# The last 512 output columns of a decode step computed with the tokens as the stationary operand

## The chip, the cores and the metric

The kernel runs on one core of a Trainium2 chip. A core has TensorE (PE in the profile; PEld is its loading of the stationary operand), VectorE (DVE), ScalarE (ACT), GpSimd (POOL) and SyncE (SP), which run side by side and wait for each other by semaphores. SP, ACT and POOL also issue DMAs between HBM and the on-chip memory SBUF; all DMAs share 16 engines. Matmul results land in PSUM, in banks of 512 fp32 numbers a partition. The metric is the device time of one execution in microseconds (us); the median over a few runs is compared.

## The reference, cut to what matters

One layer with three groups of heads (short convolution, sparse attention over a paged cache, attention over a memory) is computed for 256 prompt tokens and for 8 sequences with 4 new tokens each, 288 tokens in all. What the change touches is the end:

```python
    mixed = jnp.concatenate([y_a, y_b, y_m], axis=-1)
    return x + mixed @ w_out, kv_new, win_state, conv_new

def rms_norm(x, g):
    xf = x.astype(jnp.float32)
    y = xf * lax.rsqrt(jnp.mean(xf * xf, axis=-1, keepdims=True) + NORM_EPS)
    return (y * g.astype(jnp.float32)).astype(x.dtype)

    y_prompt = rms_norm(xp, final_g)
    y_sample = rms_norm(xs, final_g)
```

`mixed` is 288 tokens by 2048, `w_out` is 2048 by 2048, and the final norm needs the sum of squares over all 2048 output columns of a token before any column of it can be scaled.

## The kernel before

**Layout.** Everything is kept with features on the 128 partitions and the 288 tokens (`NT`: 0 to 127 and 128 to 255 prompt, 256 to 287 decode) along the free dimension. A matrix product is made tile by tile: 128 output columns at a time, with the weights as the stationary operand (128x128) and the 288 tokens as the moving one. The weights come in halves of 128 x 1024 numbers, eight 128x128 blocks each, numbered `s`; `wsrc` lists them in the order in which they are used. To hold fp32 accuracy at the speed of the rounded format fp32r, each operand is split into a rounded part and a rest: `w_load` (L215, DMA from POOL, five buffers `w`), `w_hi` (L222, ACT copy to `wh`, three buffers), `w_lo` (L227, DVE subtraction to `wl`, two buffers). `product_half` (L244) then issues 24 matmuls of 288 columns for a half: high by high, high by low and low by high for eight blocks.

**Order.** There is no scheduler: instructions stand on each engine in the order in which the Python code issues them. Side work (attention of the decode tokens, residual, squares) is written as generators; `chunk` (L159) lets each that is due take one step, twice in each half.

**The output projection.** It runs in two passes over 16 tiles of 128 output columns, since half of the 2048 rows of `mixed` are ready earlier than the other half. The first pass (L1484) multiplies rows 0 to 1023 (`y1`, the split form) and ACT copies each result to `ysum` (`first_pass`, L1429). `residual` (L1434) loads the input x in six pieces through SP and DVE adds it. The second pass (L1490) multiplies rows 1024 to 2047 (`y2`); in `second_pass` (L1458) DVE adds the PSUM tile to `ysum`, ACT squares it, DVE adds the squares to `yacc`, and ACT multiplies the tile by the norm's gain `fg`, in place.

**The tail.** After the last tile the squares are summed over partitions by matmuls with a column of ones (`sum_tokens`, L1452, tile `ssqy`), `rsqrt` (L197) makes the factor of each token in one ACT and five small DVE instructions, three matmuls (`spread_tokens`) spread the 288 factors over all partitions (tile `rb`), and DVE multiplies `ysum` by them in seven pieces (`OUT_PIECES`); each piece is stored as soon as it is done, from ACT and SP in turn (L1500 to L1503). `busy` (L1443) issues matmuls whose results nobody reads.

Of the kernel before, what the change touches and what calls it, by code (L numbers as in the profile page):

```python
# [9 lines left out]
F32 = mybir.dt.float32  # L10
# [8 lines left out]
D = 2048  # L19
KT = 16  # L20
# [49 lines left out]
DIRECT = 4  # L70
WARM = 3
LOW_FIRST = 22
TAIL_BUSY = (5, 7)
OUT_PIECES = (1, 2, 2, 3, 3, 3, 2)


@with_exitstack
def decode_step(ctx, tc, xT, xN, xD, memT, cst, w_in, w_mem, w_out, w_bg, pt, ptv, ckc, ckk, ckv, wk, wv, mk, mv,
                o_y, o_kv, o_mem, o_conv, o_wk, o_wv):
    nc = tc.nc  # L80
    pool = lambda name, bufs, **kw: ctx.enter_context(tc.tile_pool(name=name, bufs=bufs, **kw))
# [28 lines left out]
    def matmul(out, a, b, **kw):  # L110
        n = size(out)
        k, t = ((0, n / 2400 + 0.0115) if b.dtype == F32R else (1, n * 0.00048 + 0.008) if out.shape[0] == 32
                else (2, max(0.21, n * 0.00143)))
        if k != kind[0]:
            at[0] += 0.2 if 1 in (k, kind[0]) else 0.08
        kind[0] = k
        at[0] += t
        nc.tensor.matmul(out, a, b, **kw)  # L118
# [37 lines left out]
    def spawn(gen, delay=0):  # L156
        live.append([now[0] + delay, gen])
# [22 lines left out]
    def small(w, name, bufs=2):  # L180
        return psm.tile([128, w], F32, name=name, tag=name, bufs=bufs)
# [9 lines left out]
    def C(name):  # L191
        o, w = _COFF[name]
        return c[:, o:o + w]

    ident = C("ident")

    def rsqrt(r, ssq):  # L197

        v, t = small(3, "yv", 1)[:, :r.shape[1]], small(3, "yt", 1)[:, :r.shape[1]]
        act.activation(r, ssq, AF.Sqrt, scale=1.0 / D, bias=C("eps"))  # L200
        vec.tensor_scalar(v, ssq, 1.0 / D, EPS, op0=ALU.mult, op1=ALU.add)
# [9 lines left out]
    wsrc += [half(w_out[i], j) for j in range(2) for i in range(16)]  # L211
    raws, his, los = {}, {}, {}
    NH = len(wsrc)

# [12 lines left out]
    def w_lo(s, eng=None):  # L227
        if DIRECT <= s < NH and s not in los:
            los[s] = pw.tile([128, 1024], F32R, name=f"wl{s}", tag="wl", bufs=WL)
            (eng or vec).tensor_tensor(los[s], raws.pop(s), his[s].bitcast(F32), op=ALU.subtract)  # L230
# [1198 lines left out]
    def first_pass(n, z):  # L1429
        act.activation(ysum[:, n, :], z, AF.Copy)  # L1430
        return
        yield

    def residual():  # L1434
        for n in range(0, 16, 3):
            m = min(3, 16 - n)
# [6 lines left out]
    def busy(n):  # L1443

        for _ in range(n):
            matmul(rb[:, :NT], y2[:, 0, 0:128], y2[:, 0, :], start=True, stop=True)

    acc = zt("C", "yacc")
    rb = pss.tile([128, 512], F32, name="rb", tag="s")
    ssq = pss.tile([128, 512], F32, name="ssqy", tag="s")  # L1450

    def sum_tokens(sq, first):  # L1452
        for i, (o, _) in enumerate(GROUPS):
            matmul(ssq[:, i:i + 1], sq[:, o:o + 128], C("ones"), start=(first and i == 0), stop=(not first and i == 2),
                   skip_group_check=True)


    def second_pass(n, z):  # L1458
        y = ysum[:, n, :]
        vec.tensor_tensor(y, z, y, op=ALU.add)  # L1460
        if n < 15:
            yield 1
        if n == 0:
            act.activation(acc, y, AF.Square)
        else:
            s = zt("B", "ysq")
            if n < 15:
                act.activation(s, y, AF.Square)
                vec.tensor_tensor(acc, acc, s, op=ALU.add)
            else:  # L1470
                act.activation(s[:, :128], y[:, :128], AF.Square)
                vec.tensor_tensor(s[:, 128:], y[:, 128:], y[:, 128:], op=ALU.mult)
                busy(TAIL_BUSY[0])
                sum_tokens(s, False)
# [3 lines left out]
        if n == 14:  # L1478
            yield 1
            sum_tokens(acc, True)  # L1480

    spawn(split_prompt(), 2)
    spawn(split_decode(), 1)
    for n in range(16):  # L1484
        if n == 12:
# [4 lines left out]
    for n in range(16):  # L1490
        then(second_pass(n, product([(lambda j: y2[:, j, :], lambda j: y2[:, 8 + j, :])], NT)))
    while live:
        idle()

    r = small(3, "yr")
    rsqrt(r, ssq[:, 0:3])
    busy(TAIL_BUSY[1])
    spread_tokens(rb, r, GROUPS)
    n = 0
    for i, m in enumerate(OUT_PIECES):  # L1500
        yv = ysum[:, n:n + m, :]
        vec.tensor_tensor(yv, yv, rb[:, :NT].unsqueeze(1).to_broadcast([128, m, NT]), op=ALU.mult)
        (nc.sync if i % 2 else nc.scalar).dma_start(o_y[:, n:n + m, :], yv)  # L1503
        n += m

# [47 lines left out]
def _inputs(x_prompt, x_sample, cache_kv, cache_win, state_conv, cache_mem, page_table, mem_prompt,  # L1553
# [17 lines left out]
    wcat = np.concatenate([q, mq] + parts + conv + [mg, ng], 1)  # L1571
    wbg = np.concatenate([bg, np.zeros((D, 8), w.dtype)], 1).reshape(KT, 128, 32).transpose(1, 0, 2)
    wo = np.concatenate([w_out[0][0:512], w_out[0][1536:2048], w_out[0][512:1536]], 0)
    ck = cache_kv[0]
    ckc = ck[:, :, 0:2].transpose(0, 4, 2, 3, 1).reshape(160, 128, 512)
    ckk = ck[:, :, 2].transpose(0, 3, 2, 1).reshape(160, 128, 256)
# [10 lines left out]
    return dict(xT=A(tr(x)), xN=A(x[:NTP]), xD=A(x[NTP:].reshape(NTS, 4, 512).transpose(1, 0, 2).reshape(128, 512)),  # L1587
                memT=A(np.concatenate([vec(mem_norm_g), tr(mem_prompt.reshape(256, D)).reshape(128, KT * 256)], 1)), cst=A(cst), w_in=A(_ktiles(wcat)),
                w_mem=A(_ktiles(w_mem_kv[0])), w_out=A(_ktiles(wo)), w_bg=A(wbg), pt=A(pt), ptv=A(ptv), ckc=A(ckc), ckk=A(ckk), ckv=A(ckv),
                wk=A(wk), wv=A(wv), mk=A(mk), mv=A(mv))  # L1590


_OUTS = dict(o_y=(128, KT, NT), o_kv=(12, 128, NT), o_mem=(8, 128, 256), o_conv=(128, 72), o_wk=(4, 2, 128, 1024),
             o_wv=(2, 4, 128, 1024))


def _outputs(r):
    y = r["o_y"].transpose(1, 0, 2).reshape(D, NT)
# [7 lines left out]
    return (A(y[:, :NTP].T).reshape(1, NTP, D), A(y[:, NTP:].T).reshape(8, 4, D), A(kv[:NTP, 0:4])[None, None],  # L1606
            A(kv[:NTP, 4:6])[None, None], A(conv[0:2])[None, None],
            A(r["o_mem"].reshape(2, 4, 128, 256).transpose(3, 0, 1, 2))[None, None],
            A(kv[NTP:, 0:4]).reshape(1, 8, 4, 4, 2, 128), A(win)[None], A(conv[2:18]).reshape(1, 8, 2, 512))
# [15 lines left out]
```

## Time and profile before

| what | us |
|---|---|
| runs | 617.47, 617.70, 618.82; median 617.7 |
| the profiled execution, as timed | 617.0 |
| its span from first to last instruction | 614.7 |
| TensorE busy, of the span | 600.8 (98%) |
| VectorE busy | 459.1 (75%) |
| ScalarE busy | 285.8 (46%) |
| mean granted TensorE clock | 0.992 |

The span is that of the core's instructions and DMAs; 2.3 us of the timed execution lie outside it. Busy time counts an instruction from its start to its end, so that overlapping instructions of a pipeline are counted once; a matmul's own duration in the profile is longer than the distance to the next one. In rows of the trace in order of time the columns are the start, the duration of the row, engine, source line, operation, output and inputs, tile sizes, and xN for the number of instruction records in it. A matmul on plain fp32 operands leaves two records, one on fp32r operands one.

### The profile page before, as it was taken

To read this page: it belongs to the slowest core of one execution; us is meant where nothing else is said; L and a number is where in the kernel's file an instruction comes from. 1 tells how busy PE (TensorE), PEld (TensorE's weight loads), DVE (VectorE), ACT (ScalarE), POOL (GpSimd) and SP (SyncE) were. 2 spreads that over 40 slices of the span, in tenths; PEclk is the share of its full clock that TensorE was granted. 3 is DMA by queue.
4 is the path that set the end of the run, shared out by engine and by line. 5 is a ranking of instruction groups with operands and counts; after the bars stand their busy time and mean duration, and the time that the engine had idled before them with its cause. 6 is when DMAs were issued, how large, how long until landed. Compare 5 with 4: busy or idle time off the path is not lost.

```text
span 614.7 us, 13334 instructions
## 1 busy us (share of the span) xinstructions
PE 600.8 (98%) x4893; PEld 558.6 (91%) x4893; DVE 459.1 (75%) x737; ACT 285.8 (46%) x500; POOL 200.8 (33%) x282
## 2 busy tenths in 40 slices
PE   8999999999999999999999999999999999999993
PEld 6999999989999999888998989889898898999993
DVE  5789799988576599997987879897568533357754
ACT  4755545544464345325435434443544444346650
POOL 2012545434235342324465523331212364122200
PEclk8999999999999999999999999999999999999998
DMA  8999798999988998898888898989898888677623
GB/s 315 388 405 401 255 326 306 333 297 378 338 266 305 347 399 341 295 384 293 292 314 275 312 361 279 304 284 337 290 362 327 326 290 307 227 256 280 231 85 154
DMA packets 75217, 188.40 MB, mean 307 GB/s; under 512 B 8784, under 2 KB 26352, under 8 KB 74896
## 3 DMA queue, kind: packets, MB, share of 16 engines
q0 software_dynamic: 26048, 100.48, 45.5%
q1 hardware_dynamic: 47808, 84.98, 38.9%
q10 hardware_dynamic: 1296, 2.11, 0.9%
q8 instruction: 38, 0.62, 0.4%
q14 instruction: 27, 0.22, 0.1%
HBM read 182.31 MB, written 13.60 MB: 319 GB/s over the span
## 4 chain that ended last, share of the span: by engine, by line
PE 84%; DVE 7%; DMA 6%; issue 1%; SPq 1%; ACT 0%; ACTq 0%; DVEq 0%
PE z L118 65%; PE od L118 3%; DMA st<-ckc 3%; PE sk L118 3%; PE zf L118 2%; DVE pooled L135 2%; PE acc L118 2%; PE s L118 2%; DMA rx<-xT 1%; DVE wl L135 1%; DVE st L135 1%; PE pt L123 1%; DVE ysum L135 1%; DMA mraw<-memT 1%; PE pv L123 1%
## 5 line engine op out<-in xcount | busy, mean ns | idle before, releaser
L118 PE MATMUL z<-x,wh 128*128 128x288 f32 x1664 | 254.4, 302 | 0.0
L135 DVE TENSOR_TENSOR wl<-w,wh 128x1024 fp32r<-128x1024 f32 x148 | 185.6, 1255 | 86.4 <-PE z L118 43.4
L118 PEld LDWEIGHTS z<-x,wh 128*128 128x128 f32 x1664 | 229.8, 188 | 7.8 <-issue 6.1
L135 ACT ACTIVATE wh<-w 128x1024 fp32r<-128x1024 f32 x148 | 154.4, 1052 | 20.3 <-PE z L118 14.4
L118 PE MATMUL z<-x,wl 128*128 128x288 f32 x832 | 127.0, 295 | 0.3 <-DVE wl L135 0.3
L118 PEld LDWEIGHTS z<-x,wl 128*128 128x128 f32 x832 | 115.7, 188 | 0.5 <-DVE wl L135 0.5
L350 POOL TENSOR_TENSOR st<-st,cst 128x512 f32<-128x512 f32 x63 | 69.7, 1108 | 129.5 <-issue 58.5
L219 POOL DMA_DIRECT2D w<-w_in x104 | 58.2, 560 | 108.6 <-DVE wl L135 79.2
L135 DVE TENSOR_REDUCE pooled<-st 128x16 f32<-128x1024 f32 x63 | 76.2, 1210 | 5.8 <-POOL st L350 5.8
L135 DVE TENSOR_TENSOR st<-st,cst 128x512 f32<-128x512 f32 x63 | 43.8, 697 | 8.8 <-DMA st<-ckc 8.7
L219 POOL DMA_DIRECT2D w<-w_out x32 | 17.5, 550 | 64.4 <-DVE wl L135 43.6
L578 POOL DMA_INDIRECT st<-ckv,rows_v x26 | 27.0, 1040 | 32.2 <-PE od L118 17.6
L118 PE MATMUL z<-y,wh 128*128 128x288 f32 x256 | 37.0, 297 | 0.0
L118 PE MATMUL z<-y1a,wh 128*128 128x288 f32 x224 | 35.4, 298 | 0.0
L118 PEld LDWEIGHTS z<-y,wh 128*128 128x128 f32 x256 | 35.1, 188 | 0.0
L118 PEld LDWEIGHTS z<-y1a,wh 128*128 128x128 f32 x224 | 31.4, 188 | 2.1 <-issue 1.2
L118 PE MATMUL z<-m,wh 128*128 128x256 f32 x192 | 27.3, 287 | 0.5 <-DVE mvt L135 0.5
L135 ACT ACTIVATE P<-P,nm 128x128 f32<-128x128 f32 (+1 forms) x32 | 14.2, 446 | 27.7 <-DVE nm L135 27.7
L118 PEld LDWEIGHTS z<-m,wh 128*128 128x128 f32 x192 | 24.7, 191 | 0.8 <-issue 0.7
L135 ACT ACTIVATE ysum<-z 128x288 f32<-128x288 f32 x16 | 6.6, 412 | 35.2 <-PE z L118 33.4
L118 PE MATMUL z<-y,wl 128*128 128x288 f32 x128 | 19.6, 296 | 0.0
L118 PE MATMUL z<-y1a,wl 128*128 128x288 f32 x128 | 19.5, 295 | 0.0
(286 smaller groups left out, 692.0 us busy)
## 6 DMA issues: line engine op xcount, KB each, us to landing
w<-w_in POOLq DMA_DIRECT2D x104, 512.0 KB
st<-ckc SPq DMA_DIRECT2D x126, 256.0 KB, 5.5
w<-w_out POOLq DMA_DIRECT2D x32, 512.0 KB
st<-ckk SPq DMA_DIRECT2D x112, 128.0 KB, 4.9
w<-w_mem SPq DMA_DIRECT2D x12, 512.0 KB
o_wk<-wk POOLq DMA_DIRECT2D x8, 512.0 KB
o_wv<-wv POOLq DMA_DIRECT2D x8, 512.0 KB
st<-mv SPq DMA_DIRECT2D x7, 512.0 KB, 7.8
```

The lines of the kernel that those rows point to most:

```text
L118: nc.tensor.matmul(out, a, b, **kw)
L123: nc.tensor.transpose(out, a, b)
L135: return getattr(self.engine, name)(*args, **kw)
L219: (nc.gpsimd if s >= ON_SYNC else nc.sync).dma_start(raws[s], wsrc[s])
L350: done.append(eng.tensor_tensor(tm[:, :, kv], tm[:, :, kv], acmp[:, kv].unsqueeze(1).unsqueeze(1).to_broadcast([128, 2, 4, 64]), op=ALU.mu ...
L578: nc.gpsimd.indirect_dma_start(t, None, ckv, bass.IndirectOffsetOnAxis(ap=rows_v[:, j * 4 + b:j * 4 + b + 1], axis=0))
```

## The change

The last 512 output columns (4 of the 16 tiles) are taken out of both passes, which now run over `DT` = 12 tiles.

- **First pass.** After 12 tiles, `first_rows` makes the product of `y1` with the last 512 columns: the stationary operand is a 128x128 block of tokens, the moving one is 512 columns of the weights. `rows` issues six matmuls of 512 columns for a half of the weights and a group of 128 tokens; there are four halves and the two prompt groups. DVE adds the residual, which is loaded in this layout into `ysum` ahead of time (`xL`). The decode tokens are left out here.
- **Second pass.** After 12 tiles the same is done with `y2`, group 0 first. Each prompt group then has its own sum of squares (the 12 tiles by `yacc` as before, the 512 columns by an ACT square that also sums along the row), its own `rsqrt`, its own spreading matmul, four scaled pieces (three on DVE with four tiles each, one on ACT with the 512 columns) and four stores.
- **Decode tokens.** Their 32 rows of the last 512 columns are computed at the end in plain fp32, from unsplit weights, by 64 matmuls that write 32 partitions and 128 columns each (`decode_rows`; tile `zd`, 4 quarters of the columns on 4 quarters of the partitions). Four weight halves of the first pass are loaded again for it, into buffers `st` that the attention no longer uses; the other four are still in `w`.
- The output array has another layout in HBM, group by group; the host side puts it together.

```diff
+    def first_rows():
+        z = row_tiles()
+        y = y1["hi"], y1["lo"]
+        for p in range(4):
+            s, w = next_weights()
+            for g in range(2):
+                rows(z[g], w, 2 * p, y, g, p == 0, p == 3)
...
+    def rows(z, w, k, y, g, first, last):
+        wh, wl = w
+        hi, lo = y
+        mm = [(a(k + i)[:, 128 * g:128 * g + 128], w[:, i * ROWS:(i + 1) * ROWS])
+              for a, w in ((hi, wh), (lo, wh), (hi, wl)) for i in range(2)]
+        for i, (a, b) in enumerate(mm):
+            matmul(z, a, b, start=first and i == 0, stop=last and i == 5)
...
-    for n in range(16):
-        if n == 12:
-            spawn(residual())
+    for n in range(DT):
+        if n == 8:
+            nc.sync.dma_start(yl, xL)
         then(first_pass(n, product([(y1["hi"], y1["lo"])], NT)))
+    spawn(residual())
+    first_rows()
...
+    for n in range(DT):
+        if n in (2, 3, 4, 5):
+            wr[n - 2] = buffers[n - 1]
+            nc.sync.dma_start(wr[n - 2], wsrc[NH - 20 + n - 2])
+        elif n == 6:
+            nc.sync.dma_start(buffers[0][:, :640], fgl)
+        then(second_pass(n, product([y2hl], NT)))
...
+    def decode_rows(a, b):
+        for k in range(a, b):
+            for q in range(4):
+                o = (k % 2) * ROWS + 128 * q
+                matmul(zd[32 * q:32 * q + 32, :128], mixed[:, k, 256:NT], wr[k // 2][:, o:o + 128],
+                       start=(k == 0), stop=(k == KT - 1), skip_group_check=True)
...
+    squares(0, z[0])
+    gains(0)
+    r0 = factors(0, sums2[:, 0:1])
+    scale_rows(0, r0, nc.sync)
+    rows(z[1], ws[0], 2, y, 1, False, False)
+    rows(z[1], ws[1], 4, y, 1, False, False)
+    spread_rows(0, r0)
+    rows(z[1], ws[2], 6, y, 1, False, True)
+    scale_tiles(0, 0, 4, nc.sync)
+    scale_tiles(0, 4, 8, nc.sync)
+    squares(1, z[1])
+    scale_tiles(0, 8, 12, nc.sync)
+    gains(1)
+    r1 = factors(1, sums2[:, 1:2])
+    scale_rows(1, r1, nc.scalar)
+    decode_rows(0, SPREAD_AT)
+    spread_rows(1, r1)
+    decode_rows(SPREAD_AT, KT)
+    scale_tiles(1, 0, 4, nc.sync)
+    squares(2, zd[:, :128])
+    busy(TAIL_BUSY[0])
+    matmul(ssq[:, 3:4], sel, sums2[:, 2:3], start=True, stop=True)
+    scale_tiles(1, 4, 8, nc.sync)
+    gains(2)
+    scale_tiles(1, 8, 12, nc.sync)
+    r2 = factors(2, ssq[:, 3:4])
     busy(TAIL_BUSY[1])
-    spread_tokens(rb, r, GROUPS)
...
+    spread_rows(2, r2)
+    scale_rows(2, r2, nc.scalar)
+    scale_tiles(2, 0, 12, nc.sync)
```

`squares` adds a finished PSUM group to `ysum` (DVE) and squares it with a sum (ACT); `gains` multiplies by the gain (DVE); `factors` is `rsqrt`; `scale_rows` scales the 512 columns on ACT and stores them; `scale_tiles` scales four tiles on DVE and stores them.

On TensorE, at the end of the program, these instructions stood last before the change (`z` is the PSUM tile, the number behind `wh` and `wl` tells one half of the weights from another, `y` is y2):

```order
L118 MATMUL z_7556<-y_6383,wh_7487 128x288 x16
L118 MATMUL z_7556<-y_6383,wl_7525 128x288 x8
L118 MATMUL z_7588<-y_6383,wh_7523 128x288 x12
L118 MATMUL ssqy<-cst,yacc 128x1 x3
L118 MATMUL z_7588<-y_6383,wh_7523 128x288 x4
L118 MATMUL z_7588<-y_6383,wl_7557 128x288 x8
L118 MATMUL rb<-y_6383 128x288 x5
L118 MATMUL ssqy<-cst,ysq 128x1 x3
L118 MATMUL rb<-y_6383 128x288 x7
L118 MATMUL rb<-cst,yr 128x128 x2
L118 MATMUL rb<-cst,yr 128x32
```

On TensorE, from the last three halves of group 0 and group 1 on, there now stand these (`zr_0` and `zr_1` are the two groups' PSUM tiles, `zd` the decode tokens', `idl` the tile that nobody reads):

```order
L120 MATMUL ssqy<-cst,both 128x1
L120 MATMUL zr_0_7434<-wh_7464,y_6383 128x512 x4
L120 MATMUL zr_0_7434<-wl_last,y_6383 128x512 x2
...
L120 MATMUL rb<-cst,yr_7496 128x128
L120 MATMUL zr_1_7435<-wh_7464,y_6383 128x512 x4
L120 MATMUL zr_1_7435<-wl_last,y_6383 128x512 x2
L120 MATMUL zd<-st_105,mixed 32x128 x8
...
L120 MATMUL zd<-w_7316,mixed 32x128 x4
L120 MATMUL rb<-cst,yr_7535 128x128
...
L120 MATMUL zd<-w_7352,mixed 32x128 x8
L120 MATMUL idl<-y_6383 128x288 x4
...
L120 MATMUL rb<-cst,yr_7625 128x32
```

The one spreading of factors behind all products has become three: group 0's stands ahead of group 1's last half, group 1's inside the decode tokens' matmuls, and only that of the decode tokens' 32 factors stands last.

On VectorE the program ended so before (`wl` is the subtraction for the last half, `ysum<-ysum,rb` the scaling of the output):

```order
L135 TENSOR_TENSOR wl_7557<-w_7406,wh_7523 128x1024
L135 TENSOR_TENSOR ysum<-z_7556,ysum 128x288
L135 TENSOR_TENSOR yacc<-yacc,ysq 128x288
L135 TENSOR_TENSOR ysum<-z_7588,ysum 128x288
L135 TENSOR_TENSOR ysq<-ysum 128x160
L135 TENSOR_SCALAR yv<-ssqy 128x3
L135 RECIPROCAL yr<-yr 128x3
...
L135 TENSOR_TENSOR ysum<-ysum,rb 128x288
L135 TENSOR_TENSOR ysum<-ysum,rb 128x576 x2
L135 TENSOR_TENSOR ysum<-ysum,rb 128x864 x3
L135 TENSOR_TENSOR ysum<-ysum,rb 128x576
```

On VectorE the stretch from group 1's factors to the end now reads (`yo` and `yod` are the output buffers, `st_104` holds the gains):

```order
L137 SCALAR_TENSOR_TENSOR yr_7535<-yt,yr_7535 128x1
L137 TENSOR_TENSOR yo<-ysum,rb 128x512
L137 TENSOR_TENSOR ysum<-zd,ysum 128x128
L137 TENSOR_TENSOR yo<-ysum,rb 128x512
L137 TENSOR_TENSOR yod<-ysum,st_104 128x128
L137 TENSOR_TENSOR yo<-ysum,rb 128x512
L137 SCALAR_TENSOR_TENSOR yv<-ssqy,yrest 128x1
L137 RECIPROCAL yr_7625<-yr_7625 128x1
L137 TENSOR_TENSOR yt<-yr_7625 128x1
L137 SCALAR_TENSOR_TENSOR yt<-yt,yv 128x1
L137 SCALAR_TENSOR_TENSOR yr_7625<-yt,yr_7625 128x1
L137 TENSOR_TENSOR yod<-ysum,rb 128x384
```

Two of group 1's three scalings now stand between the decode tokens' sum and their factors; behind the factors there is one multiplication of 384 columns in place of seven over 4608.

On SyncE's queue, behind the loads of the attention, there stand now:

```order
L1505 DMA ysum<-xL 128x1152
L1444 DMA xr_6917<-xT 128x864
L1444 DMA xr_6957<-xT 128x864
L1444 DMA xr_7006<-xT 128x864
L1516 DMA st_105<-w_out 128x1024
L1444 DMA xr_7081<-xT 128x864
L1516 DMA st_106<-w_out 128x1024
L1516 DMA st_107<-w_out 128x1024
L1516 DMA st_108<-w_out 128x1024
L1518 DMA st_104<-fgl 128x640
```

Before, six pieces of x stood there alone; the four reloaded halves and the gains are new, and two pieces of x have become `xL`.

More of the change, by code (lines that the diff above doesn't have):

```diff
@@ L210, in decode_step @@
     wsrc[:4] = [wsrc[i] for i in (0, 2, 1, 3)]
-    wsrc += [half(w_out[i], j) for j in range(2) for i in range(16)]
+    for j in range(2):
+        wsrc += [half(w_out[i], j) for i in range(DT)] + [half(w_out[DT + 2 * j + i // 2], i % 2) for i in range(4)]
     raws, his, los = {}, {}, {}
@@ L1441, in residual, with next_weights, row_tiles @@
             yield 1
-    def busy(n):
-        for _ in range(n):
-            matmul(rb[:, :NT], y2[:, 0, 0:128], y2[:, 0, :], start=True, stop=True)
-    acc = zt("C", "yacc")
[L1449 to L1455, printed above, removed]
+    yl = ysum[:, DT:, :].rearrange("p k n -> p (k n)")
+    part = (yl[:, 0:ROWS], yl[:, ROWS:2 * ROWS], yl[:, 2 * ROWS:])
+    def rows(z, w, k, y, g, first, last):
[5 more added lines that the diff above has]
+            matmul(z, a, b, start=first and i == 0, stop=last and i == 5)
+    def next_weights():
+        s = nhalf[0]
+        nhalf[0] += 1
+        w_hi(s + 2)
+        w_lo(s + 1)
+        return s, (his.pop(s), los.pop(s))
+    def row_tiles():
+        return [pz.tile([128, ROWS], F32, name=f"zr{nhalf[0]}_{g}", tag="z") for g in range(2)]
+    def first_rows():
[5 more added lines that the diff above has]
+                rows(z[g], w, 2 * p, y, g, p == 0, p == 3)
+                if g == 1:
+                    w_load(s + WR + 1)
+                if p == 3:
+                    vec.tensor_tensor(part[g], z[g], part[g], op=ALU.add)
+                chunk()
+    acc = zt("C", "yacc")
     def second_pass(n, z):
@@ L1460, in second_pass @@
         vec.tensor_tensor(y, z, y, op=ALU.add)
-        if n < 15:
-            yield 1
+        yield 1
         if n == 0:
@@ L1466, in second_pass @@
             s = zt("B", "ysq")
[L1467 to L1474, printed above, removed]
+            act.activation(s, y, AF.Square)
+            vec.tensor_tensor(acc, acc, s, op=ALU.add)
@@ new lines, in decode_step, with busy @@
+    rest, sums2 = small(3, "yrest", 1), small(3, "ysums", 1)
+    quarters = small(32, "imp", 1)
+    both = zt("A", "both")
+    sel, accd = both[:, 0:128], both[:, 128:256]
+    by4 = lambda t: t.rearrange("p (q t) -> p q t", t=32)
+    vec.tensor_reduce(quarters, ident.rearrange("p (q t) -> p t q", t=32), axis=AX.X, op=ALU.add)
+    vec.tensor_copy(by4(sel), quarters.unsqueeze(1).to_broadcast([128, 4, 32]))
+    def busy(n):
+        for _ in range(n):
+            matmul(idl[:, :NT], y2[:, 0, 0:128], y2[:, 0, :], start=True, stop=True)
@@ new lines, in gains, with factors, spread_rows, scale_rows @@
+    def gains(g):
+        vec.tensor_tensor(out[g][:, out[g].shape[1] - part[g].shape[1]:], part[g], fgr[g], op=ALU.mult)
+    def factors(g, ssq):
+        r = small(1, f"yr{g}", 1)
+        rsqrt(r, ssq, rest[:, g:g + 1])
+        return r
+    def spread_rows(g, r):
+        n, k = (128, 128) if g < 2 else (32, 32)
+        matmul(rb[:, g * 128:g * 128 + n], r[:k].to_broadcast([k, 128]), ident[:k, :n], start=True, stop=True)
+    def scale_rows(g, r, eng):
+        w = part[g].shape[1]
+        o = out[g].shape[1] - w
+        act.activation(out[g][:, o:], out[g][:, o:], AF.Copy, scale=r)
+        eng.dma_start(o_y[:, g * 2048 + o:g * 2048 + o + w], out[g][:, o:])
@@ new lines, in scale_tiles @@
+    def scale_tiles(g, a, b, eng):
+        n = 128 if g < 2 else 32
+        yv = out[g][:, a * n:b * n]
+        vec.tensor_tensor(yv.rearrange("p (m t) -> p m t", t=n), ysum[:, a:b, g * 128:g * 128 + n],
+                          rb[:, g * 128:g * 128 + n].unsqueeze(1).to_broadcast([128, b - a, n]), op=ALU.mult)
+        eng.dma_start(o_y[:, g * 2048 + a * n:g * 2048 + b * n], yv)
+    for p in range(4):
+        wr[4 + p] = raws[NH - 4 + p]
+    y = y2hl
+    s, w4 = next_weights()
+    rows(z[0], w4, 0, y, 0, True, False)
@@ L1492, in decode_step @@
+    chunk()
+    rows(z[1], w4, 0, y, 1, True, False)
+    w_hi(s + 3)
+    w_lo(s + 2)
+    los[s + 3] = pbig.tile([128, 1024], F32R, name="wl_last", tag="big")
+    vec.tensor_tensor(los[s + 3], wr[7], his[s + 3].bitcast(F32), op=ALU.subtract)
+    chunk()
     while live:
         idle()
-    r = small(3, "yr")
-    rsqrt(r, ssq[:, 0:3])
-    busy(TAIL_BUSY[1])
-    spread_tokens(rb, r, GROUPS)
[L1499 to L1504, printed above, removed]
+    vec.tensor_copy(by4(accd), acc[:, 256:NT].unsqueeze(1).to_broadcast([128, 4, 32]))
@@ new lines, in decode_step @@
+    ws = [(his.pop(s + i), los.pop(s + i)) for i in (1, 2, 3)]
+    rows(z[0], ws[0], 2, y, 0, False, False)
+    rows(z[0], ws[1], 4, y, 0, False, False)
+    for i, a in enumerate((acc[:, 0:128], acc[:, 128:256], accd)):
+        matmul(ssq[:, i:i + 1], a, C("ones"), start=True, stop=True, skip_group_check=True)
+    rows(z[0], ws[2], 6, y, 0, False, True)
+    vec.tensor_scalar(rest, ssq[:, 0:3], 1.0 / D, EPS, op0=ALU.mult, op1=ALU.add)
+    squares(0, z[0])
+    gains(0)
+    r0 = factors(0, sums2[:, 0:1])
```

65 lines of the change are left out of this document (45 added, 20 removed).

## The prediction

> **What bounds the kernel now.** I read the page's busy times first, then the chain of work that ended last, then the rows in order of time over the two passes and the tail.
>
> ```profile
> span 614.7 us, 13334 instructions
> PE   600.8 (98%) x4893; PEld 558.6 (91%) x4893; DVE 459.1 (75%) x737; ACT 285.8 (46%) x500; POOL 200.8 (33%) x282
> ...
> 539.93 59.03 PE z L118 x443
> 598.96 0.76 PE ssqy L118 x6
> 599.72 1.70 PE z L118 x12
> ...
> 606.36 4.22 DVE ysum L135 x5
> ```
>
> TensorE's products are the chain without a gap for the last 59 us of the passes, and the chain leaves TensorE only after them. So there are two ways to gain: fewer TensorE cycles in the passes, and a shorter tail. To price the passes, I take the distance between tiles, not a matmul's own duration, since matmuls overlap.
>
> ```profile
> 41.39 2.08 PE L118 MATMUL z<-m,wh 128*128 128x256 f32 x16
> ...
> 44.27 2.08 PE L118 MATMUL z<-m,wh 128*128 128x256 f32 x16
> ...
> 536.38 1.95 PE L118 MATMUL z<-y1a,wh 128*128 128x288 f32 x13
> ...
> 549.18 2.33 PE L118 MATMUL z<-y,wh 128*128 128x288 f32 x16
> ...
> 587.60 2.29 PE L118 MATMUL z<-y,wh 128*128 128x288 f32 x16
> ...
> 590.80 2.29 PE L118 MATMUL z<-y,wh 128*128 128x288 f32 x16
> ```
>
> 24 matmuls of 288 columns take 590.80 - 587.60 = 3.20 us, 133.3 ns each. 24 of 256 columns take 2.88 us, 120.0 ns each. The difference is 0.417 ns a column. The four tiles of the first pass that the change takes away lie from 536.38 to 549.18: 12.80 us. The 13th tile of the second pass starts at 587.60, and I call this moment T; from T to the span's end are 27.1 us.
>
> ```profile
> 603.16 0.26 ACT L135 ACTIVATE yr<-ssqy,cst 128x3 f32<-128x3 f32 x1 [0.27 <-PE ssqy L118]
> 603.45 0.16 DVE L135 TENSOR_SCALAR yv<-ssqy 128x3 f32<-128x3 f32 x1 [1.20 <-ACT yr L135]
> ...
> 604.12 0.16 DVE L135 SCALAR_TENSOR_TENSOR yr<-yt,yr 128x3 f32<-128x3 f32 x1
> 604.34 0.85 PE L118 MATMUL rb<-cst,yr 128*128 128x128 f32 x6 [0.19 <-DVE yr L135]
> 605.24 5.34 DVE L135 TENSOR_TENSOR ysum<-ysum,rb 128x288 f32<-128x288 f32 x7 [0.95 <-PE rb L118]
> 605.72 5.27 ACTq L1503 DMA_DIRECT2D o_y<-ysum  x4
> ...
> 612.00:613.00 1.00, 0.00 (x0) 0.00 (x0) 0.00 (x0) 0.00 (x0) 0.00 (x0) 0.50 0.96 371
> 613.00:614.00 1.00, 0.00 (x0) 0.00 (x0) 0.00 (x0) 0.00 (x0) 0.00 (x0) 0.50 0.04 14
> ...
> DMA to landing us min/median/max: 1.8/1.8/1.8
> ```
>
> The tail is serial: factors, spreading, 5.34 us of scaling, and the stores behind it. VectorE is done at 610.58, but the DMAs move at 371 GB/s (last column of the rows by stretch) until 613, and the span ends 1.65 us after the last bytes. The first store had free engines and landed 1.8 us after its issue.
>
> **The first pass.** Four halves with two groups of six matmuls are 48 of 512 columns. No row has this width on fp32r operands. By the line through the two widths above one takes 120.0 + 256 x 0.417 = 226.7 ns, and 48 take 10.88 us against 12.80: **-1.9 us**. Bounds for one: 133.3 ns, the widest row of this kind, and 483 ns, a record of the widest plain fp32 row:
>
> ```profile
> L118 PE MATMUL acc<-PT,qk 128*128 128x512 f32 x24 | 11.6, 592 | 0.0
> L118 PE MATMUL z<-y,wh 128*128 128x288 f32 x256 | 37.0, 297 | 0.0
> L135 DVE TENSOR_TENSOR wl<-w,wh 128x1024 fp32r<-128x1024 f32 x148 | 185.6, 1255 | 86.4 <-PE z L118 43.4
> L135 ACT ACTIVATE wh<-w 128x1024 fp32r<-128x1024 f32 x148 | 154.4, 1052 | 20.3 <-PE z L118 14.4
> ```
>
> I take the line, since both fp32r widths lie on it at one column a cycle of the granted clock of 1.00 and the fp32 row is another number format. The Trainium skill, "TensorE: Matmul & The Clock Gate", section "Back-to-back issue gap", gives columns / 2.4 + 2.5 ns for a warm clock, which is 215.8 ns here, and for the 96 wide matmuls of both passes the sum would come out 1.05 us lower; but for 256 columns it gives 109.2 ns where this trace has 120.0, so the measurement decides.
>
> The other engines keep up. A half now takes 12 x 226.7 = 2.72 us instead of 3.20; DVE needs 1.26 us for its `wl` and ACT 1.05 us for its `wh`. The two additions of 512 columns and the loads of x fall into DVE's free time. `xL` and the first x pieces are issued long before, as two of the six x loads were; the fourth x piece still waits for a buffer of y1, and its addition stands three tiles into the second pass, with some 10 us to arrive. Uncovered, one such load would cost about 4 us.
>
> **The second pass up to T** keeps its twelve tiles of 3.20 us. New are three reloaded weight halves, a load of x and the gains on SP in one burst, 2.3 MB, at its start (a fourth half goes ahead).
>
> ```profile
> 550.00:560.00 10.00, 10.00 (x77) 10.00 (x76) 5.67 (x9) 5.08 (x9) 2.12 (x4) 1.00 0.91 342
> 560.00:570.00 10.00, 10.00 (x77) 10.00 (x76) 7.94 (x12) 6.21 (x10) 2.59 (x5) 1.00 0.62 219
> ...
> 550.96 0.55 POOL L219 DMA_DIRECT2D w<-w_out  x1 [2.16 <-DVE wl L135]
> ```
>
> The DMA engines are 91% and 62% busy there. About 0.9 MB of the burst were there before as x, so 1.4 MB come on top, about 4 us at 342 GB/s. The weights of the passes have a lead: `w` issued at 550.96 is converted four tiles later, 11 us on. I cost the burst at nothing; without that lead it would be up to 4 us.
>
> **From T on, along the path.**
>
> 1. TensorE, prompt groups: 48 wide matmuls, 10.88 us. In them stand the three sums `ssqy`, 0.69 us by the rows below (598.89 to 599.58), and one spreading of 128 factors, a third of the 0.85 us above: 0.28. That is T + 11.85. Two hand-overs are close: DVE still has the last tile's work and three `wl` of 1.26 us at T, and by my count each is done 0.3 to 1.5 us before TensorE reaches it.
> 2. The factors of group 0 cost nothing here: its product ends at T + 7.5; addition 0.2 + 0.69, square 0.62 and reading the sum 0.19, then 1.12 us for `rsqrt`, about T + 10.25, when TensorE has just done two more halves of group 1 (T + 10.2). The stores and scalings of group 0 lie under group 1's and the decode tokens' matmuls.
> 3. Decode rows: 64 matmuls with 32 output partitions and 128 columns.
>
> ```profile
> 453.14 0.61 PEld L118 LDWEIGHTS sn<-qk,qz 128*32 128x32 f32 x32
> ...
> 489.67 1.50 PE L118 MATMUL od<-st,S 128*32 128x256 f32 x24
> 490.99 0.61 PE L118 MATMUL od<-qk,S 128*32 128x256 f32 x8
> ...
> 598.89 0.83 PE L118 MATMUL ssqy<-cst,yacc 128*128 128x1 f32 x6
> 599.55 0.57 PEld L118 LDWEIGHTS z<-y,wh 128*128 128x128 f32 x4
> 599.58 0.77 PE L118 MATMUL z<-y,wh 128*128 128x288 f32 x4
> ...
> L135 DVE TENSOR_TENSOR P<-s,cst 128x512 f32<-128x512 f32 x12 | 8.2, 686 | 1.7 <-PE s L118 1.6
> L135 ACT ACTIVATE st<-st 128x512 f32<-128x512 f32 x1 | 0.6, 617 | 0.0
> L135 ACT ACTIVATION_READ_ACCUMULATOR st<-st 128x1 f32 x5 | 1.0, 191 | 0.0
> ```
>
>  The `od` rows are 16 such matmuls (two records each) of 256 columns in 490.99 + 0.61 - 0.07 - 489.67 = 1.86 us, 116 ns each; the `sn` rows 16 of 32 columns in 0.61 us, 38 ns each. Half of the wide one is 58, the line between both 71; I take 64 ns: 4.1 us, bounds 2.4 and 7.4. With the spreading of group 1 (its factors ready at T + 14.8, TensorE gets there at T + 15.2) the decode product ends at T + 16.25.
> 4. DVE, 0.2 later: adding the decode tile (128 columns, about 0.3), a piece of 512 columns, the gains, another piece, 0.6 + 0.2 + 0.6 (the 4608 columns above took 5.34 us, 1.16 ns each): T + 18.15. ACT's square, the sum on TensorE and the square root (some 1.1 us) hide under these pieces; without the pieces they would cost the same, so little could be won by moving them.
> 5. The five small DVE steps, 603.45 to 604.28: 0.85. Spreading 32 factors, from 604.28 to 605.24 for three, about 0.4 for one. The last multiplication, 384 columns, 0.55. T + 19.95.
> 6. The last stores are 64 and 192 KB with nothing queued ahead: 0.08 to issue, 1.8 to land as the first store of 144 KB did, and 1.05 to the span's end (that store's bytes were gone about 0.6 us before it landed, and 1.65 - 0.6 = 1.05). T + **22.9**, against T + 27.1: **-4.2 us**.
>
>  The Trainium skill, "DMA: Bandwidth & Descriptors", section "Anatomy of one DMA — SWDGE (gpsimd) path", fits 2.0 us + bytes / 436e3 to transfers that GpSimd issues, which would be 2.45 us for the last store, and the time would be 0.65 us higher; these stores come from ACT and SP, and for 144 KB it gives 2.34 us where this trace has 1.8, so the row stands.
>
> Sum: -1.9 - 4.2 = -6.1 us. The profiled execution took 617.0 us (span 614.7 and 2.3 around it), which is 0.7 below the median of 617.7; applied to it, 610.9, and to the median **611.6 us**.
>
> **The rivals.**
>
> - *Slower: the decode matmuls do not run side by side.* If the four quarters of `zd` go one after the other, a matmul costs what a plain fp32 one costs, 2 records x 483 ns for 512 columns, 242 ns for 128: 15.5 us instead of 4.1, +11.4, **623.0 us**. It turns the result from 160 ns a matmul on (64 + 6100 / 64). Against it: `od` has the same shape of output and takes 116 ns for twice the columns. For it: there the quarters have other moving data and wider tiles, and no row has 128 columns. Chance 0.05.
> - *The burst makes weights late.* The 11 us of lead are not enough while SP's and POOL's loads share the engines and the copies of the window caches go on: 1.5 to 3 us of stall in the second pass, **613.1 to 614.6**. Against it, the second half of the stretch is 62% busy. 0.10.
> - *VectorE's queue sets the tail.* From T + 7.7 on it is nearly full, and all three groups' chains stand in one order. If each of the eight small waits costs 0.3 more, the groups slip by 2.4 us: **614.0**. 0.10.
> - *The change gives back what it gains,* for instance by a hand-over of about 1.5 us in both passes and a tail that is only 3 us shorter: **617.6**. Nothing in the rows points to it. 0.04.
> - *Wide matmuls cost less than their columns.* If 512 columns cost what 288 do, 96 x (226.7 - 133.3) = 9.0 us more are gained, **602.6**. Against it is the slope of one column a cycle. 0.02. (The section on the back-to-back gap named above also states about 131 ns as sustained at 512 columns; the 120.0 ns of 256 columns speak against it here.)
>
> **How the numbers follow.** The forecast as worked out, 610 to 613, has 0.69. The likeliest gives 611.6. The lower end of the range is the decode bound of 2.4 us, worth only about 0.7 since DVE then holds the path, and matmuls some 10 ns shorter, worth 1: 610.0. The upper one is the decode bound of 7.4 us, +3.3, which takes in the two slips: **610.0 to 615.0**. Outside lie the slow rival, the null and the cheap one, and some of the slips, about 0.13. A difference of 0.2% (1.2 us) is about what runs of this kernel can tell from none, by their spread of 1.35 us. Faster by more: 0.69 + 0.10 + 0.10 + 0.02 = 0.91, less 0.01 for slips that add up: 0.90. Within: 0.04. Slower: 0.06.
>
> **What would show it.** Between the wide matmuls of one tile 227 ns and no waits for `wl`; the second pass starting 1.9 us earlier; in it no ACT wait for `w`; `zd` in 4.1 us, 64 ns a matmul; group 0's spreading waiting less than 0.2 us; between the end of `zd` and the last multiplication 3.7 us with VectorE busy for most; the last store issued at T + 20 and the span ending 3 us later. The prediction fails if any of the three unseen costs (wide fp32r matmul, 128-column decode matmul, burst of loads) lies near its far bound.

## The result, and the profile after

| | before | after |
|---|---|---|
| median of the runs, us | 618.48 (22 runs) | 615.23 (22 runs) |
| ratio of after to before, 95% interval | | 0.9934 (0.9908 to 0.9960) |
| span of the profiled execution | 614.7 | 614.4 |

The ratio is that of the means of the runs, 619.5 and 615.4 us, where one slow run of after (620.68 us) is left out; the two medians lie 3.3 us apart. By the ratio the change makes the kernel 4.1 us faster (2.5 to 5.7 by the interval). Forecast were 6.1 us, so the sign and two thirds of the size came out. The two profiled spans differ by only 0.3 us, and the first thing to learn is why that is no contradiction.

The page of the changed kernel, its span and the busy times:

```profile
span 614.4 us, 13419 instructions
...
PE 603.0 (98%) x4919; PEld 554.0 (90%) x4919; DVE 461.0 (75%) x749; ACT 285.3 (46%) x499; POOL 200.5 (33%) x282
```

TensorE is as full as before. For a comparison of the changed part alone I need a mark that both programs pass just ahead of it. The last transposition `ot` ahead of the first pass's last 512 columns is one. Its row in the timeline of before (start, duration, engine and line, names, tiles), and below it the same of after:

```profile
536.36 0.27 PE L123 MATMUL ot<-cst,odr 128*128 128x128 f32 x1
```

```profile
541.53 0.27 PE L125 MATMUL ot<-cst,odr 128*128 128x128 f32 x1
```

I call this moment M. This one execution of after was 5.2 us late at M, before any changed instruction on TensorE; from M to the span's end it needs 614.4 - 541.5 = 72.9 us, before 614.7 - 536.4 = 78.3. So the changed part is **5.4 us shorter**, and in this pair of executions what lies ahead of it is longer. Below, "behind M" is always the span's end less M.

The chain of waits of after, from M on (start, length, what):

```profile
541.80 11.17 PE zr L120 x48
552.97 38.41 PE z L120 x288
591.38 5.58 PE zr L120 x24
596.96 0.56 PE ssqy L120 x6
597.52 4.29 PE zr L120 x18
601.81 0.40 PE rb L120 x2
602.21 1.40 PE zr L120 x6
603.61 2.98 PE zd L120 x104
606.59 0.42 PE rb L120 x2
607.00 0.84 PE zd L120 x24
607.84 0.02 issue
607.86 0.29 DVE ysum L137
...
610.76 0.55 DVE yod L137
```

The reader sees three things. TensorE holds the chain without a gap to the end of `zd`: the 48 wide matmuls of the first pass in 11.17 us (12.80 before, for four tiles), twelve tiles in 38.41 us, 3.20 each as before, the prompt groups, and the decode rows. VectorE then holds it for 3.5 us, with one spreading of 0.42 us on TensorE in between, where before it was 5.34 us of scaling behind a serial sum. And TensorE ends its products later than before, seen from M: in after at about 607.7, where `idl<-y` begins, whose results nobody reads, that is M + 66.2; before at 601.2 or M + 64.9, where the first such matmuls (`rb<-y`) begin:

```profile
601.24 0.82 PE L118 MATMUL rb<-y 128*128 128x288 f32 x5
```

The whole gain is in what stands behind the products: 614.4 - 607.7 = 6.7 us, where it was 13.4. This part is the timeline of after:

```profile
591.22 1.09 PE L120 MATMUL zr<-wh,y 128*128 128x512 f32 x4
...
601.72 0.49 PE L120 MATMUL rb<-cst,yr 128*128 128x128 f32 x2
...
603.54 1.95 PE L120 MATMUL zd<-st,mixed 128*32 128x128 f32 x64
...
606.51 0.49 PE L120 MATMUL rb<-cst,yr 128*128 128x128 f32 x2
...
607.73 0.80 PE L120 MATMUL idl<-y 128*128 128x288 f32 x4
607.86 0.29 DVE L137 TENSOR_TENSOR ysum<-zd,ysum 128x128 f32<-128x128 f32 x1
...
608.87 0.68 DVE L137 TENSOR_TENSOR yo<-ysum,rb 128x512 f32<-128x512 f32 x1
...
609.47 0.15 DVE L137 SCALAR_TENSOR_TENSOR yv<-ssqy,yrest 128x1 f32<-128x1 f32 x1
...
610.32 0.40 PE L120 MATMUL rb<-cst,yr 32*128 32x32 f32 x2 [0.39 <-DVE yr L137]
...
610.76 0.55 DVE L137 TENSOR_TENSOR yod<-ysum,rb 128x384 f32<-128x384 f32 x1 [0.49 <-PE rb L120]
611.34 0.33 SPq L1578 DMA_DIRECT2D o_y<-yod  x1
```

Here T, the start of the second pass's last 512 columns, is 591.22, and the span ends at T + 23.2; the forecast had T + 22.9. The rows are taken up one by one in the section on why.

### The profile page after: what moved, and what is told of

It is laid out like the page before. It is cut to its first block, busy times and chain, and to the rows that moved or that the text cites. A ratio compares the mean times of both kernels' runs of the same rounds, so it can differ in the third digit from the quotient of the medians.

```text
span 614.4 us, 13419 instructions
## 1 busy us (share of the span) xinstructions
PE 603.0 (98%) x4919; PEld 554.0 (90%) x4919; DVE 461.0 (75%) x749; ACT 285.3 (46%) x499; POOL 200.5 (33%) x282
## 4 chain that ended last, share of the span: by engine, by line
PE 78%; DMA 11%; DVE 8%; issue 2%; SPq 1%; ACT 0%; ACTq 0%; DVEq 0%
PE z L120 56%; DMA st<-ckc 5%; PE zr L120 4%; PE od L120 3%; DMA st<-ckk 3%; PE sk L120 3%; PE zf L120 2%; DVE wl L137 2%; DVE pooled L137 2%; PE acc L120 2%; PE s L120 2%; DMA rx<-xT 1%; DVE st L137 1%; PE pt L125 1%; DMA mraw<-memT 1%
## 5 line engine op out<-in xcount | busy, mean ns | idle before, releaser
L120 PE MATMUL z<-y,wh 128*128 128x288 f32 x192 | 27.6, 297 | 0.0
L120 PE MATMUL z<-y1a,wh 128*128 128x288 f32 x168 | 26.7, 299 | 0.0
L120 PEld LDWEIGHTS z<-y,wh 128*128 128x128 f32 x192 | 26.3, 188 | 0.1
L120 PEld LDWEIGHTS z<-y1a,wh 128*128 128x128 f32 x168 | 23.6, 188 | 2.1 <-issue 1.2
L120 PE MATMUL sk<-st,qz 128*32 128x256 f32 x272 | 20.4, 383 | 1.4 <-DMA st<-ckk 1.2
L120 PE MATMUL od<-st,S 128*32 128x256 f32 x256 | 18.7, 382 | 0.0
L120 PE MATMUL zf<-mixed,w 128*128 128x256 f32 x64 | 16.6, 421 | 1.9 <-DVE mixed L137 1.7
```

## The experiments

Three questions were open. Which part of the change brings the 5.4 us (the first four experiments)? What does a wide matmul cost, since the first pass gained less than forecast (the fifth)? And where are the 1.3 us lost that lie between 5.4 behind M and 4.1 over all (the others)? For the last question the theories are: A, nothing is lost, single executions only scatter at M; B1, the two new inputs `xL` and `fgl` shift the arrays behind them in HBM, and the part ahead of M pays; B2, two more inputs cost time wherever they are declared.

**The changed kernel again**, nothing edited.

> The changed kernel once more, unchanged. The mark M is the last small transposition ot, which stands just ahead of the place where the first wide matmuls start; L is the span from M to the end, 78.3 us before the change and 72.9 after it in the two profiles. Theory A (the gain is local: 1.55 us in the first pass, 3.9 us behind the twelfth tile of the second pass, and what lies ahead of M only scatters): L is 72.9 within 0.2 us again while M moves by 1 us or more, and the ratio to before is about 0.991 (617.7 - 5.5). Theory B (the changed program loses 1 to 2 us ahead of M): L the same, but M again about 5 us later than the 536.4 us of before, and a ratio near 0.994.

614.33 us (12 runs), ratio 0.9936 (0.9904 to 0.9969); span 610.7, M at 537.8, so 72.9 behind M. The part behind M repeats to 0.1 us, while M itself came 3.7 us earlier than in the first profile. So the length behind M can be read from one profile, and M can't. The ratio lies nearer to theory B's 0.994 than to A's 0.991, but its interval holds both, and B's M of about 541 did not come.

**The first pass undone.** Its last 512 columns are made by tiles of 288 tokens as before, and the wide load `xL` is left out; the second pass adds to what that leaves, so the last 512 output columns lack the residual and mix two layouts.

```diff
-        if n == 8:
-            nc.sync.dma_start(yl, xL)
...
-    first_rows()
+    for n in range(DT, 16):
+        then(first_pass(n, product([(y1["hi"], y1["lo"])], NT)))
```

> The first pass undone: four tiles of 288 columns in place of the 48 wide matmuls (the residual of the last 512 columns is left out and their values are not the reference's), all else as changed. Theory A: L is 1.55 us longer, 74.4 us, the gap from M to the second pass 12.8 us. Rival (the wide matmuls buy nothing, since the hand-over between the passes takes it back): L stays at 72.9.

614.93 us (10 runs), ratio 0.9950 (0.9911 to 0.9990). In its timeline the mark, and the start of the second pass:

```profile
539.42 0.27 PE L125 MATMUL ot<-cst,odr 128*128 128x128 f32 x1
...
552.25 2.33 PE L120 MATMUL z<-y,wh 128*128 128x288 f32 x16
```

The four tiles take 12.8 us again, and 613.9 - 539.4 = 74.5 us lie behind M, 1.6 more than with the wide matmuls. So the wide first pass is worth 1.6 us, not the 1.9 forecast.

**All factors behind the decode rows.** The three groups' `rsqrt`, spreading, scaling and stores stand behind the last `zd` matmul; the products are as in the changed kernel, and the additions, squares and gains of the two prompt groups still lie under matmuls.

```diff
-    r0 = factors(0, sums2[:, 0:1])
-    scale_rows(0, r0, nc.sync)
...
-    decode_rows(0, SPREAD_AT)
-    spread_rows(1, r1)
-    decode_rows(SPREAD_AT, KT)
-    scale_tiles(1, 0, 4, nc.sync)
+    decode_rows(0, KT)
...
+    r0 = factors(0, sums2[:, 0:1])
+    r1 = factors(1, sums2[:, 1:2])
     r2 = factors(2, ssq[:, 3:4])
+    for g, r in enumerate((r0, r1, r2)):
+        spread_rows(g, r)
+    for g, r in enumerate((r0, r1, r2)):
+        scale_rows(g, r, nc.scalar)
+        for n in range(0, 12, 4 if g < 2 else 12):
+            scale_tiles(g, n, n + (4 if g < 2 else 12), nc.sync)
```

> The same products in the same order, but the factors, their spreading, all scaling and all stores stand behind the decode tokens' matmuls, as before the change. Theory A (the tail is shorter because two groups' scaling and stores lie under later matmuls): TensorE ends its products at the same place or 0.5 us earlier, and the span ends 3 to 4.5 us later, L 76 to 77.4 us. Rival (the tail is shorter because the second pass has fewer TensorE cycles): less than 1 us longer, L below 73.9.

617.31 us (10 runs), ratio 0.9994 (0.9953 to 1.0035); span 615.0, 77.2 behind M. Its timeline, at the end of the decode rows and on VectorE:

```profile
601.16 1.93 PE L120 MATMUL zd<-w,mixed 128*32 128x128 f32 x64
603.02 0.79 PE L120 MATMUL idl<-y 128*128 128x288 f32 x4
```

```profile
606.85 3.67 DVE L137 TENSOR_TENSOR yo<-ysum,rb 128x512 f32<-128x512 f32 x6 [0.49 <-PE rb L120]
610.45 0.55 DVE L137 TENSOR_TENSOR yod<-ysum,rb 128x384 f32<-128x384 f32 x1
```

TensorE is done 1.0 us earlier (M + 65.2), since no spreading stands in its way, but the 3.67 us of scaling come behind the last factors in one row, and the end 12.0 us behind TensorE. 4.3 us of the 5.4 go, and 1.1 stay behind M. With the same products and the same layout nothing measurable is left of the gain over whole runs: it is the order by groups, which lets factors, scaling and stores run under matmuls, that pays for the change.

**The quarters of the decode rows in turn.** All 16 matmuls of one quarter of the columns, then those of the next.

```diff
-        for k in range(a, b):
-            for q in range(4):
+        for q in range(4):
+            for k in range(a, b):
```

> The 64 decode matmuls with the loops turned: all steps of one quarter of the columns, then the next quarter, so that neighbouring matmuls write the same 32 partitions. If the four quarters run side by side because neighbours lie on different partitions, each matmul now costs what a plain fp32 one of 128 columns costs, about 240 ns in place of 57: 15.5 us for the 64, L about 84.8 us, a slower kernel than before the change. If the order does not matter: 57 ns, L 72.9 us.

One run: 623.39 us; span 621.6, 80.8 behind M, 7.9 more than the changed kernel. The starts of the quarters in its timeline:

```profile
602.77 1.93 PE L120 MATMUL zd<-st,mixed 128*32 128x128 f32 x16
604.54 0.93 PE L120 MATMUL zd<-w,mixed 128*32 128x128 f32 x7
605.20 0.30 PE L120 MATMUL zd<-st,mixed 128*32 128x128 f32 x1
605.31 0.27 PE L120 MATMUL zd<-w,mixed 128*32 128x128 f32 x1
...
614.96 0.79 PE L120 MATMUL idl<-y 128*128 128x288 f32 x4
```

From 602.77 to 614.96, less 0.42 of spreading between them, are 184 ns for each of the 64, against 59 in the changed kernel (603.54 to 607.73, less 0.42). Matmuls on different quarters do run side by side, and the order by `k` outside and `q` inside is what lets them. My price for the slow rival was too high, though: eight matmuls of one quarter alone take 1.77 us, 221 ns each, but at 605.20 the first of the next quarter (`st` again) already runs between the last of the old one, and that saves the rest.

**The width of an fp32r matmul.** Behind the end of the changed kernel stand blocks of 16 equal matmuls on operands of the kernel, of 256 to 512 columns, each block between 24 of 288 columns; two more blocks of 512 columns have weights as the stationary operand, a new block each time and then always the same one. The time of the whole says nothing.

```diff
+    wa, wb = ws[2][0], ws[1][0]
+    for n in (256, 288, 320, 384, 448, 512):
+        busy(24)
+        for i in range(16):
+            matmul(idl[:, :n], y2[:, i, 0:128], wa[:, 0:n], start=True, stop=True)
+    busy(24)
+    for i in range(16):
+        matmul(idl[:, :512], wb[:, 128 * (i % 8):128 * (i % 8) + 128], wa[:, 0:512], start=True, stop=True)
+    busy(24)
+    for i in range(16):
+        matmul(idl[:, :512], wb[:, 0:128], wa[:, 512:1024], start=True, stop=True)
```

> The changed kernel with blocks of 16 matmuls on fp32r behind its last store, tokens as the stationary operand and 256, 288, 320, 384, 448 and 512 columns of weights moving, then 16 of 512 columns with a weight block as the stationary operand, then 16 with one and the same stationary block; their results are not read, and the time of the whole says nothing. The changed kernel's own wide matmuls stand 234 ns apart, where the line through 256 and 288 columns gave 226.7. Theory C (a column costs more in wide matmuls, whatever the operands): the distance leaves the line between 288 and 512 columns in all three forms, 234 ns at 512. Rival D (the tokens as the stationary operand cost it): 227 ns with a weight block or a constant block. Rival E (it is the running kernel, other engines reading the same memory): 227 ns in all forms here, since nothing else runs.

Rows of its timeline; the next row's start ends a block:

```profile
613.55 2.06 PE L120 MATMUL idl<-wh,y 128*128 128x256 f32 x16
615.44 3.32 PE L120 MATMUL idl<-y 128*128 128x288 f32 x24
618.60 2.28 PE L120 MATMUL idl<-wh,y 128*128 128x288 f32 x16
620.72 3.32 PE L120 MATMUL idl<-y 128*128 128x288 f32 x24
...
641.77 3.88 PE L120 MATMUL idl<-wh,y 128*128 128x512 f32 x16
645.49 3.33 PE L120 MATMUL idl<-y 128*128 128x288 f32 x24
648.65 3.81 PE L120 MATMUL idl<-wh,wh 128*128 128x512 f32 x16
652.30 3.32 PE L120 MATMUL idl<-y 128*128 128x288 f32 x24
655.46 3.84 PE L120 MATMUL idl<-wh,wh 128*128 128x512 f32 x16
```

16 of 256 columns take 1.89 us, 118 ns each; of 288 2.12, 132.5; of 512 3.72, 232.5. With VectorE and ScalarE idle, the wide matmul costs what it costs in the kernel (11.17 us / 48 = 233), so other engines are not to blame (E). With a new weight block each time it takes 228. The last block has no row behind it; a row is 0.16 us longer than the distance to the next in the other two blocks of 512 columns, so it took about 3.68 us by this estimate, 230 ns each. So 2.5 to 4.5 of the 5.8 ns above the forecast 226.7 go with the tokens as the stationary operand (D), and the rest would be with the columns (C): neither theory alone fits, since C expected 234 in all three forms and D 227 in the last two. Among the blocks with tokens as the stationary operand a column costs (232.5 - 118.1) / 256 = 0.447 ns, where my two points had 0.417; the same two widths of this experiment give 0.45 and 233 ns at 512.

**The kernel before, with two more inputs** of the sizes of `xL` and `fgl` that nothing reads, declared where the change declares them; then the kernel before unchanged, as a control; then the changed kernel with `xL` and `fgl` declared behind all other inputs.

```diff
-def decode_step(ctx, tc, xT, xN, xD, memT, cst, w_in, ...
+def decode_step(ctx, tc, xT, xN, xD, xL, fgl, memT, cst, w_in, ...
```

> The kernel before the change with two more input arrays of the size of xL and fgl, which it does not read; they stand between the same arrays as in the changed kernel, so that everything behind them lies elsewhere in HBM. L is as before, 78.3 us. Theory B1 (the changed program loses 1 to 2 us ahead of M because the arrays lie elsewhere): M is later and the ratio to before about 1.0025 to 1.003. Theory A (only scatter): ratio 1.000.

> The kernel before the change, unchanged, as a control: ratio 1.000 with an interval that shows what the comparison can tell, and a second profile of it. L 78.3 us. Theory A: M anywhere between 536 and 542 us as in the profiles of the changed kernel (537.8 to 541.5). Theory B: M below 538.

> The changed kernel with xL and fgl declared behind all other inputs, so that the other arrays lie where they lay before the change. L 72.9 us. Theory B1: the loss ahead of M is gone, ratio 0.990 to 0.991. Theory A: the ratio stays within 0.001 of that of the changed kernel, 0.9934.

Two more inputs: 620.50 us (12 runs), ratio 1.0031 (0.9999 to 1.0063). The control: 618.57 (12 runs), 1.0001 (0.9971 to 1.0032). The changed kernel with its inputs behind: 611.92 (9 runs), 0.9900 (0.9868 to 0.9933). All three ratios fell where B1 put them. The single profiles didn't follow: M was 539.8, 539.3 and 542.8, where B expected less than 538 for the control and no loss for the last. And the differences are as small as the intervals, and one control is missing, the unread inputs behind all others. The next four runs have it, beside a repeat of the rest.

> The changed kernel with its two new inputs declared behind all others, a second time. Theory B1 (where the other arrays lie in memory costs about 1.6 us ahead of the last 512 columns): ratio to before about 0.990 to 0.991, and below that of the changed kernel as it is in the same job by about 0.0026. Theory A (placement costs nothing, the earlier 0.990 was scatter): the same ratio as the changed kernel, 0.993 to 0.994.

> The kernel before with two unread inputs at the places of the new ones, a second time. Theory B1: ratio about 1.0026 (1.6 us of 618). Theory A: 1.000.

> The kernel before with the same two unread inputs, but declared behind all others. Theory B1 (the place of the other arrays): 1.000. Theory B2 (two more inputs cost time wherever they are declared): about 1.0026, as with them at the front. Theory A: 1.000.

> The changed kernel, unchanged, a third time, in the same job as the three above. Theory B1: ratio 0.993 to 0.994, above the version with its new inputs behind the others by about 0.0026. Theory A: equal to that version.

The changed kernel with its inputs behind: 614.38 us (11 runs), ratio 0.9922 (0.9891 to 0.9953). The unread inputs at the front: 620.49 (12 runs), 1.0019 (0.9987 to 1.0050). Behind: 620.07 (12 runs), 1.0016 (0.9989 to 1.0042). The changed kernel: 615.32 (12 runs), 0.9936 (0.9903 to 0.9969).

The repeat takes away B1's best point: the advantage of the inputs behind shrank from 0.0036 to 0.0014, and the unread inputs cost about the same behind as in front. To use all runs at once, I take the span of each and subtract the length behind M of its kernel (72.9 us for the changed one, in five profiles between 72.8 and 72.9; 78.5 for the one before, in five between 78.3 and 78.7). What is left is M, with its standard error:

| kernel | runs | M, us |
|---|---|---|
| before | 97 | 538.4 ± 0.2 |
| before, two unread inputs in front | 24 | 539.7 ± 0.4 |
| before, two unread inputs behind | 12 | 539.3 ± 0.5 |
| changed | 44 | 540.4 ± 0.3 |
| changed, its inputs behind | 19 | 539.2 ± 0.5 |

The changed kernel reaches M 2.0 ± 0.4 us later than the one before: theory A falls. Within the two sets of runs that have the spans of both kernels side by side it is 1.3 ± 0.8 (with the first experiment) and 1.9 ± 0.7 (with the last), 1.6 ± 0.5 together. Two inputs that nothing reads, wherever they are declared, bring 1.2 ± 0.4 in the kernel before (36 runs with them, mean 539.6). That is a sum over many runs: the interval of each of the three comparisons holds 1.000, and the changed kernel was not run without them, so that they bring as much there is not shown. Whether they stand in front or behind changes M by 0.3 ± 0.6 in the kernel before and by 1.2 ± 0.6 in the changed one; that decides neither for B1 nor for B2, and whether the version with the inputs behind is better than the changed kernel stays open as well.

The profiles narrow the place. The transposition `ot` runs twice (its row by tile has the durations, then the first and the last start), in before and in after:

```profile
L123 PE MATMUL ot<-cst,odr x2: 270/271/272, 369.1 to 536.4; 128*128 128x128 f32 x2
```

```profile
L125 PE MATMUL ot<-cst,odr x2: 270/271/272, 374.3 to 541.5; 128*128 128x128 f32 x2
```

From the first to the second, M, are 167.2 us in each of the 14 profiles. So all scatter and all loss lie ahead of the first `ot`. The traces of before and after hold the same instructions ahead of M but for one, the load `xL`, which is issued at 489.3, inside the stretch that never changes. What the changed kernel loses there is therefore not the work of an instruction that the change added.

## Why the prediction was right, and where it was not

Forecast -6.1 us; measured behind M -5.4 to -5.6, ahead of M +2.0, around the span -0.2 (1.8 us lie outside it, 1.9 before, as means of the runs), which makes -3.8 over all runs and agrees with the -4.1 of the first comparison. By the steps:

1. **What bounds the kernel** was right: TensorE without a gap, then a serial tail. The gain also divides much as its terms say: they put the end of the products 0.7 us later than before (T + 16.25 less the 1.9 of the first pass, against T + 13.64) and the tail behind them 6.8 us shorter; measured are 1.3 later and 6.7 shorter.
2. **The wide matmuls** were mis-sized: 227 ns forecast, 232.5 to 234 measured (in the timeline of after the first wide matmul of the first pass starts at 541.56 and the second pass at 552.81: 11.25 us, 234 ns for each of 48). The step that failed is the line through 256 and 288 columns, taken from two stages with weights as the stationary operand: over a distance of 32 columns an error of one nanosecond is stretched sevenfold on the way to 512. With tokens as the stationary operand the fifth experiment has 118.1 for 256 columns where the forecast used 120.0, and the line comes out at 233. The first pass brings -1.55 where -1.9 was forecast, and the second pass loses 0.3 in the same way. The Trainium skill, "TensorE: Matmul & The Clock Gate", section "Back-to-back issue gap", would give an estimate of 215.8 ns by its formula for a single isolated matmul; the fifth experiment has 232.5, so it lies further off than my line, on the same side; the 131 ns that the section calls sustained at 512 columns is not seen here at all.
3. **The burst of loads costs nothing**: right. The chain has 288 matmuls in 38.41 us, and no wait in them.
4. **The factors of group 0 are hidden**: right. Its spreading starts at T + 10.5 (forecast: the factors at T + 10.25); the matmul ahead of it, the last of six that began at 600.25, ends at about 601.65, so TensorE waits some 0.07 us. The third experiment prices the hiding of all groups' factors, scaling and stores together: 4.3 us.
5. **Decode rows**: 57 ns each over the first 52 (603.54 to 606.51), where 64 ns were forecast; with the spreading they end at T + 16.5 instead of T + 16.25, since the prompt groups ahead of them ended 0.5 us later than forecast, 0.3 of it in the wide matmuls. The slow rival did not come true; its mechanism is real, as the fourth experiment shows for quarters in turn, at a price of 184 ns instead of 242.
6. **VectorE's steps** were right one by one: the addition 0.29 (0.3 forecast), pieces to T + 18.3 (18.15), five small steps 0.8 (0.85), spreading 0.44 (0.4), last multiplication 0.55 (0.55). The last store leaves at T + 20.1 (19.95).
7. **The last store** was right in its sum: 3.06 us from issue to the span's end, 2.93 forecast. The stores of 256 KB landed later than the 1.8 us I took from one of 144 KB, by the page's DMA issues (count, KB each, median us to landing):

```profile
o_y<-yo SPq DMA_DIRECT2D x7, 256.0 KB, 2.5
...
o_y<-yo ACTq DMA_DIRECT2D x1, 256.0 KB, 3.0
```

   For the 192 KB of the last one the profile has no landing. The Trainium skill, "DMA: Bandwidth & Descriptors", section "Anatomy of one DMA — SWDGE (gpsimd) path", gives an estimate of 2.6 us for 256 KB by its fit, near these rows, though it speaks of GpSimd's transfers.
8. **What was applied to the median** is the larger miss. The sum began at the first pass's last 512 columns and put everything ahead of them at nothing; the runs show 2.0 ± 0.4 us of loss ahead of M (1.6 ± 0.5 within sets of runs), and the profiles place it ahead of the first `ot`, where the two programs have the same instructions. This is the mechanism of the rival "gives back what it gains", but at a place that none of my rivals named. Two unread inputs bring 1.2 ± 0.4 in the kernel before; whether they explain as much of it in the changed one, what the rest is (the other layouts of `w_out` and of the output in HBM and the longer program were not run alone), and by which way an unread input would cost time, stays open. The waits of TensorE don't name a place. Its longest ones on work ahead of M, in the profile of after and in that of the same kernel of the first experiment (who, for whom: us, times, longest):

```profile
PE zf L120 <- DVE mixed L137: 1.7, 2, 1.4
PE sk L120 <- DMA st<-ckk: 1.2, 1, 1.2
PE pt L125 <- DVE P L137: 1.2, 1, 1.2
```

```profile
PE zf L120 <- DVE mixed L137: 1.9, 3, 1.4
...
PE sk L120 <- DMA st<-ckk: 0.3, 1, 0.3
```

   One program waits in one execution for a cache load (`sk`) and for VectorE (`pt`) where it hardly does in another. M moved between 537.8 and 542.4 us in three profiles of the same kernel, more than these waits add up to.

The measured ratio applied to the 617.7 us from which the forecast started is 613.6 us, inside the range of 610.0 to 615.0; the median of 615.23 itself, beside a before of 618.48 in the same runs, lies 0.2 above it. That the ratio falls inside is in part luck: the range had been drawn wider on the slow side for the decode rows and the burst, which then cost nothing more, and another loss, which it did not hold, took their place.

## What to carry to other kernels

Where an end is serial behind the last product (a norm's factor, scaling, stores), cut the product so that a part of the rows is complete early, and let its factor, scaling and stores run under the matmuls of the rest: here that was worth 4.3 of 5.4 us, and TensorE ended its products 1.3 us later than before the change. Small matmuls with 32 output partitions went side by side here where neighbours in the program wrote different quarters (59 ns each, against 184 with the quarters in turn), so it pays to look at their order. And compare two profiles from a mark that both pass unchanged, while what lies ahead of the mark is compared over many runs: a single pair of spans showed 0.3 us here, the runs 4.1.

## What was not expected of the hardware

Over all runs the kernel before with two more input arrays that no instruction reads had the part ahead of M 1.2 ± 0.4 us longer (36 runs against 97), though no single comparison tells it from none, and where they are declared made no difference that the runs could tell. Between 256 and 512 columns an fp32r matmul with tokens as the stationary operand costs 0.447 ns a column at a granted clock of 1.00, not the 0.417 that two widths close together suggested. Plain fp32 matmuls of 128 columns with 32 output partitions take 57 ns when neighbours write different quarters and 221 ns when eight in a row write the same (184 on average over all 64 in that order).
